# Three of four weight sums of a seven-product pair, moved from vector additions to accumulating DMA transfers

## The chip, the cores and the metric

The kernel runs on one core of a Trainium2 chip. The metric is device time in microseconds (us). A core has a matrix engine (TensorE, PE in the profile, with its weight loads shown apart as PEld), a vector engine (VectorE, DVE), a scalar engine (ScalarE, ACT), a general engine (GpSimd, POOL) and a sync engine that issues transfers (SyncE, SP). Each engine works through its own list of instructions in order; semaphores tie the lists together. Transfers are carried out by 16 DMA engines.

## The reference, cut to what matters

The program is one step of a recurrent decoder trunk with two layers over 536 token columns (16 learned tokens, 512 prompt tokens, 8 samples). Each layer has a feed-forward block, a recurrent mixer and a second feed-forward block, so there are four feed-forward blocks in all. Only they matter here:

```
def half_ffn(x, g, w_gate, w_up, w_down):
    h = rmsnorm(x, g)
    return 0.5 * ((jax.nn.silu(h @ w_gate) * (h @ w_up)) @ w_down)

x = x + half_ffn(x, norm_ffn1, ffn1_gate, ffn1_up, ffn1_down)   # D_MODEL 1024, D_FF 2816
```

All of it is 32-bit floating point.

## The kernel before, in words

The model width of 1024 is cut into 8 blocks of 128 rows, the hidden width of 2816 into 22 tiles of 128 columns. A *pair* is one such tile of the gate weights and the same tile of the up weights, 512 KB each. To keep 32-bit accuracy every operand is split into a rounded high part and the remainder (`hi` and `lo`), and a block product is three matmuls: high by high, high by low, low by high (`block_mm`, lines 330 to 337). A weight split is a cast on ScalarE (line 292) and a subtraction on VectorE that needs the cast (line 293).

Of the 22 pairs of a block the first four are *plain* (`run_plain`). The other 18 use a scheme with *seven products* in place of eight (`run_seven`, from line 471). The width is cut into two halves of 4 blocks, the tokens into two halves of 268 columns (260 in the last block), and sums and differences of halves are multiplied: sums of the activations are made once (`prepare`, tiles `sumh` and `suml`), sums of the weights for each pair. With g0, g1 the two halves of the gate tile and u0, u1 those of the up tile, the weight operands are g0 and g1 (`w`), t1 = g0 + u0, t2 = g0 + u0 + u1, s = u0 + u1, u1, and t4 = g0 + u0 + u1 + g1. A product is 12 matmuls of 128 by 128 weights and 268 columns. In order the seven products use: g0, g1, t2, t1, u0 + u1, u1, t4. They write three PSUM banks, a, b and c: the first, third, fifth and seventh product add up in a, the second stands in b, the fourth and sixth add up in c. Between them ScalarE copies an intermediate value out of a bank (`keep`, line 490), and VectorE and ScalarE finish a part of the output (lines 502, 503, 513, 516, 519). Four PSUM banks rotate.

The sums are made by `seven_item`. In the kernel before, all four are additions on VectorE into one tile `wsum` of 4 x 512 columns: `sums_a` (lines 348 and 349) makes t1 and t2, `sums_b` (lines 354 and 355) makes u0 + u1 and t4. Splits follow: `w` (1024 columns), `t` (t2 and t1, 1024 columns), `s` (u0 + u1 and t4, 1024 columns), `u` (u1, 512 columns). `it.steps` is the list of steps that the pair before calls (`nstep`), `it.late` the list of those that the pair itself calls.

The loop over pairs alternates with the down-projection: `PIECES` cuts the 22 hidden tiles into 8, 8 and 6, and behind each piece the 8 output blocks of the down-projection run over it (`run_down`). So the pairs of seven products stand in rows of 4, 8 and 6 in each of the four blocks, 72 in all.

Weights come by `load_pair` (line 300, SyncE's queue) into tiles `raw` and `rawx`, two buffers each, so that two pairs fit at a time. High and low parts go to `whi` and `wlo` or `whix` and `wlox` (`wtile`), two buffers each; a counter assigns them in turn. A tile that is asked for again waits until a buffer of its tag has been read for the last time. The order of instructions on each engine is not that of the text alone: a planner sorts what the text emits, by priority in text order and by when it takes an instruction to be ready, and then sets the semaphores.

Of the kernel before, what the change touches and what calls it, by code (L numbers as in the profile page):

```python
# [11 lines left out]
F32 = mybir.dt.float32  # L12
# [3 lines left out]
ALU = mybir.AluOpType  # L16
# [90 lines left out]
def trunk(ctx, tc, A, O):  # L107
    nc = tc.nc
    P = 128
    cnt = [0]  # L110

    def til(pool, shape, tag, dt=F32, bufs=None):
        cnt[0] += 1
        kw = {} if bufs is None else {"bufs": bufs}
        return pool.tile(shape, dt, tag=tag, name=f"{tag}_{cnt[0]}", **kw)
# [17 lines left out]
    def bank(tag="m"):  # L133
        return til(rings[tag][0], [P, 512], tag)
# [140 lines left out]
    ext = {}  # L275
    turn = {"raw": 0, "whi": 0, "wlo": 0}

    def wtile(tag):
        n = turn[tag]
        turn[tag] = n + 1  # L280
        dt = F32 if tag == "raw" else F32R
        if ext and n % 4 > 1:
            return til(ext["pool"], [P, 2, 512], f"{tag}x", dt, bufs=2)
        return til(wpool, [P, NK, P], tag, dt, bufs=2).rearrange("p (h k) m -> p h (k m)", h=2)
# [4 lines left out]
    def split_w(src):  # L289
        n = src.shape[1]  # L290
        hi, lo = wtile("whi")[:, :n], wtile("wlo")[:, :n]
        nc.scalar.copy(hi, src)
        nc.vector.tensor_sub(lo, src, hi.bitcast(F32))  # L293
        return hi, lo

    def load_pair(it, srcs, nk):
        it.raw = [wtile("raw") for _ in srcs]
        for t, src in zip(it.raw, srcs):
            dst = t.rearrange("p h (k m) -> p (h k) m", m=P)[:, :nk]
            nc.sync.dma_start(dst, src.rearrange("(k p) m -> p k m", p=P))  # L300
# [25 lines left out]
    def pair_item(wg, wu, j):  # L326
        return plain_item([w[:, 128 * j:128 * j + 128] for w in (wg, wu)], NK)


    def block_mm(o, u, nk, rh, rl, start, stop):  # L330
        hi, lo = u
        kw = {} if start else {"skip_group_check": True}
        for k in range(nk):
            nc.tensor.matmul(o, hi[:, k], rh(k), start=start and k == 0, stop=False, **kw)  # L334
            nc.tensor.matmul(o, hi[:, k], rl(k), start=False, stop=False, **kw)  # L335
            nc.tensor.matmul(o, lo[:, k], rh(k), start=False, stop=stop and k == nk - 1, **kw)  # L336
# [3 lines left out]
    def seven_item(wg, wu, j):  # L340
        it = Item()
        it.w = {}
        it.load = lambda: load_pair(it, [w[:, 128 * j:128 * j + 128] for w in (wg, wu)], NK)

        def sums_a():
            g, u = it.raw
            it.t = t = til(ext["pool"], [P, 4, 512], "wsum", bufs=1)
            nc.vector.tensor_add(t[:, 1], g[:, 0], u[:, 0])
            nc.vector.tensor_add(t[:, 0], t[:, 1], u[:, 1])

        def sums_b():
            g, u = it.raw
            t = it.t
            nc.vector.tensor_add(t[:, 2], u[:, 0], u[:, 1])
            nc.vector.tensor_add(t[:, 3], t[:, 0], g[:, 1])

        def split(name, src):
            def fn():
                it.w[name] = split_w(src())
            return fn  # L360

        it.steps = [sums_a, split("w", lambda: it.raw[0]), split("t", lambda: it.t[:, 0:2]), sums_b]
        it.late = [split("s", lambda: it.t[:, 2:4]), split("u", lambda: it.raw[1][:, 1:2])]
        return it

    def ffn(l, pre, rstd, first=None, done=None, start=None, tokens=PARTS, scaled_end=None):
# [5 lines left out]
        n = a1 - a0  # L372
        t1, t2, tl = slice(a0, a1), slice(b0, b1), slice(a0, b1)
# [6 lines left out]
        def flush():  # L380
            while pending:
                pending.pop(0)()
# [3 lines left out]
        with tc.tile_pool(name="ffn", bufs=2) as fp:  # L386
            ext["pool"] = fp

            def gtile(dt=F32):
                return til(fp, [P, 2, T], "hid", dt, bufs=9)  # L390

            def hidden(gt, ut):
                h = gtile(F32R)
                hid.append(h)

                def fn():
                    nc.vector.tensor_mul(ut[:, tl], ut[:, tl], gt[:, tl])
                    nc.scalar.copy(h[:, 0, tl], ut[:, tl])
                    nc.vector.tensor_sub(h[:, 1, tl], ut[:, tl], h[:, 0, tl].bitcast(F32))

                pending.append(fn)
# [69 lines left out]
            def run_seven(it, j, nxt):  # L471
                gt, ut = til(fp, [P, T], "gt"), til(fp, [P, T], "ut")
                bank_of = {}

                def product(b, name, i, rh, rl, first, last):
                    if first:
                        bank_of[b] = bank("d")[:, :n]
                    u = tuple(z[:, i].rearrange("p (k m) -> p k m", m=P) for z in it.w[name])
                    block_mm(bank_of[b], u, 4, rh, rl, first, last)
                    return bank_of[b]  # L480

                def half_x(h, ts):
                    return (lambda k: hh[:, 4 * h + k, ts]), (lambda k: hl[:, 4 * h + k, ts])

                def half_s(i):
                    return (lambda k: Z["h"][:, i, k]), (lambda k: Z["l"][:, i, k])

                def keep(ps):
                    s = til(fp, [P, n], "part", bufs=4)
                    nc.scalar.copy(s, ps)  # L490
                    return s

                def nstep():
                    if nxt is not None and nxt.steps:
                        nxt.steps.pop(0)()

                pa = product("a", "w", 0, *half_x(0, t1), True, True)
                s1 = keep(pa)
                it.late[0]()
                flush()  # L500
                pb = product("b", "w", 1, *half_x(1, t1), True, True)
                nc.vector.tensor_add(gt[:, t1], pb, s1)
                nc.scalar.activation(gt[:, t1], gt[:, t1], AF.Silu)
                it.late[1]()
                pa = product("a", "t", 0, *half_s(1), False, True)
                s2 = keep(pa)
                load_next()
                nstep()
                pc = product("c", "t", 1, *half_s(0), True, True)
                s3 = keep(pc)  # L510
                nstep()
                pa = product("a", "s", 0, *half_s(2), False, True)
                nc.vector.tensor_add(ut[:, t2], pa, s3)
                nstep()
                pc = product("c", "u", 0, *half_s(3), False, True)
                nc.vector.tensor_add(ut[:, t1], pc, s2)
                nstep()
                pa = product("a", "s", 1, *half_x(1, t2), False, True)
                nc.scalar.activation(gt[:, t2], pa, AF.Silu)
                hidden(gt, ut)  # L520

            def run_down(it, k0, k1, m0, parts, nxt):
                nk = k1 - k0
                flush()
                load_next()
                for i in range(2):
                    m = m0 + i
                    xv = X['x'][:, m]
                    for ts in parts:
                        sl = slice(*ts)  # L530
                        ps = bank("d")[:, :ts[1] - ts[0]]
                        block_mm(ps, it.w[i], nk, lambda k: hid[k0 + k][:, 0, sl], lambda k: hid[k0 + k][:, 1, sl],
                                 True, True)
                        nc.vector.scalar_tensor_tensor(xv[:, sl], ps, -0.5, xv[:, sl], ALU.mult, ALU.add)  # L534
                        if nxt is not None and nxt.steps:
                            nxt.steps.pop(0)()
                    if done is not None and k1 == FT:
                        late_done.append((m, parts[0]))
                        while len(late_done) > (2 if m < NK - 1 or parts[-1] != tokens[-1] else 0):
                            done(*late_done.pop(0))  # L540

            items = []
            for k0, k1 in PIECES:
                for j in range(k0, k1):
                    if j < PLAIN:
                        it = first if j == 0 and first is not None else pair_item(wg, wu, j)
# [20 lines left out]
            def load_next():  # L567
                if loads:
                    loads.pop(0).load()
# [1017 lines left out]

    xd = []
    ffn(0, "ffn1", rstd, first[0], spill(xd), loaded)
    rstd = norm_in("norm_mix", 0)  # L1590
    left.close()
    even_mixer(rstd, xd, left)
    psum(d=4, m=4)
    ffn(0, "ffn2", norm_rstd())
    xd = []
    ffn(1, "ffn1", norm_in("norm_ffn1", 1), done=spill(xd))
    rstd = norm_in("norm_mix", 1)
    left.close()
# [94 lines left out]
```

## Time and profile before

| | |
|---|---|
| median of 3 runs | 2301.66 us (2300.69 to 2308.91) |
| the profiled execution | 2313.27 us, its span 2311.5 us |
| mean granted TensorE clock | 0.991 of full speed |
| busy share of the span | TensorE 98%, weight loads 95%, VectorE 71%, ScalarE 47%, GpSimd 6% |
| mean DMA rate over the span | 99 GB/s |

The profile is of one execution. "Busy" is the time in which an engine had an instruction in work. In the list of a timeline, each instruction stands with its start, its duration, engine, line, operation and the tiles that it writes and reads (buffer numbers left out); in brackets stands how long the engine was idle before it and what ended that idle time.

### The profile page before, as it was taken

Reading aid. Unit: us, or ns where it says so; the run is one execution under the profiler, and the core shown is the slowest. Engines: PE = TensorE matmul, PEld = TensorE weight load, DVE = VectorE, ACT = ScalarE, POOL = GpSimd, SP = SyncE. Lnnn points to the kernel's source line nnn. Section 1 sums busy time; section 2 is a strip of 40 time slices with the busy share of each in tenths; the row PEclk is TensorE's granted clock in tenths of the full one; section 3 lists DMA queues with packets and bytes.
Section 4 is the critical chain, followed back from the end, with each engine's and each line's share of the span. In section 5 each row is a group of like instructions: output and inputs, shape, how many; then the busy total and the mean of one; then the engine's idle time right before and its main releaser. Section 6 shows DMA issues by size and latency. Waiting matters only on the chain.

```text
span 2311.5 us, 47443 instructions
## 1 busy us (share of the span) xinstructions
PE 2256.8 (98%) x19520; PEld 2206.5 (95%) x19520; DVE 1646.7 (71%) x2971; ACT 1082.8 (47%) x2056; POOL 143.5 (6%) x192
## 2 busy tenths in 40 slices
PE   8999999999999999999999999999999999999998
PEld 8999999998998888999999999999999889999998
DVE  7858576686666878966757885857666777948576
ACT  6525254374444456434535452525434464525355
POOL 0000000312212100000000000000021210000000
PEclk9999999999999999999999999999999999999999
DMA  6323334223222116242423332333434353333324
GB/s 171 106 78 101 92 92 132 81 64 94 79 71 72 49 49 167 74 119 75 118 74 101 92 110 74 101 92 94 128 110 128 111 160 92 92 92 101 110 85 136
DMA packets 409393, 229.23 MB, mean 99 GB/s; under 512 B 19252, under 2 KB 400501, under 8 KB 409176
## 3 DMA queue, kind: packets, MB, share of 16 engines
q1 hardware_dynamic: 408456, 224.78, 33.5%
q8 instruction: 153, 2.51, 0.5%
q10 hardware_dynamic: 720, 1.42, 0.2%
q14 instruction: 64, 0.52, 0.1%
HBM read 211.19 MB, written 14.97 MB: 98 GB/s over the span
## 4 chain that ended last, share of the span: by engine, by line
PE 86%; DVE 5%; DMA 3%; ACT 2%; issue 1%; POOL 1%; SPq 0%; ACTq 0%; POOLq 0%; DVEq 0%
PE d L334 21%; PE d L335 21%; PE d L336 21%; PE d L240 5%; PE d L242 4%; PE d L241 4%; PE w L1182 1%; PE w L1204 1%; DMA vb<-dv 1%; DVE wlo L229 1%; DMA raw<-in_even_w_out_dram 1%; PE m L155 1%; DMA sq<-dr 1%; DMA raw<-in_odd_w_out_dram 1%; PE w L1187 1%
## 5 line engine op out<-in xcount | busy, mean ns | idle before, releaser
L240 PE MATMUL d<-hh,whi 128*128 128x264 f32 (+2 forms) x1136 | 343.6, 303 | 2.0 <-DVE xT L596 1.3
L242 PE MATMUL d<-hh,wlo 128*128 128x264 f32 (+2 forms) x1136 | 326.7, 288 | 1.9 <-DVE wlo L229 1.7
L241 PE MATMUL d<-hl,whi 128*128 128x264 f32 (+2 forms) x1136 | 326.6, 288 | 0.5 <-DVE hl L1418 0.5
L334 PE MATMUL d<-hh,whi 128*128 128x268 f32 (+1 forms) x832 | 237.8, 286 | 1.8 <-ACT hh L187 1.3
L335 PE MATMUL d<-hl,whi 128*128 128x268 f32 (+1 forms) x832 | 238.1, 286 | 0.9 <-DVE hl L188 0.9
L336 PE MATMUL d<-hh,wlo 128*128 128x268 f32 (+1 forms) x832 | 237.7, 286 | 0.7 <-DVE wlo L293 0.7
L240 PEld LDWEIGHTS d<-hh,whi 128*128 128x128 f32 x1136 | 216.1, 190 | 7.5 <-issue 2.4
L242 PEld LDWEIGHTS d<-hh,wlo 128*128 128x128 f32 x1136 | 215.4, 190 | 4.6 <-DVE wlo L229 4.0
L241 PEld LDWEIGHTS d<-hl,whi 128*128 128x128 f32 x1136 | 216.3, 190 | 0.9 <-DVE hl L1418 0.7
L534 DVE SCALAR_TENSOR_TENSOR xT<-d,xT 128x272 f32<-128x272 f32 (+2 forms) x192 | 82.9, 433 | 166.7 <-PE d L336 166.6
L334 PE MATMUL d<-hid,whi 128*128 128x264 f32 (+2 forms) x704 | 201.5, 287 | 0.0
L334 PE MATMUL d<-hid,whix 128*128 128x264 f32 (+2 forms) x704 | 201.2, 286 | 0.0
L335 PE MATMUL d<-hid,whix 128*128 128x264 f32 (+2 forms) x704 | 200.8, 285 | 0.0
L335 PE MATMUL d<-hid,whi 128*128 128x264 f32 (+2 forms) x704 | 200.7, 286 | 0.0
L336 PE MATMUL d<-hid,wlox 128*128 128x264 f32 (+2 forms) x704 | 200.6, 285 | 0.0
L336 PE MATMUL d<-hid,wlo 128*128 128x264 f32 (+2 forms) x704 | 200.5, 286 | 0.0
L334 PE MATMUL d<-sumh,whix 128*128 128x268 f32 (+1 forms) x576 | 170.9, 297 | 0.0
L336 PE MATMUL d<-sumh,wlo 128*128 128x268 f32 (+1 forms) x576 | 164.7, 286 | 0.0
L335 PE MATMUL d<-suml,whix 128*128 128x268 f32 (+1 forms) x576 | 164.4, 285 | 0.0
L334 PE MATMUL d<-sumh,whi 128*128 128x268 f32 (+1 forms) x576 | 164.2, 285 | 0.0
L336 PE MATMUL d<-sumh,wlox 128*128 128x268 f32 (+1 forms) x576 | 164.0, 285 | 0.0
L335 PE MATMUL d<-suml,whi 128*128 128x268 f32 (+1 forms) x576 | 164.0, 285 | 0.0
(383 smaller groups left out, 6557.8 us busy)
## 6 DMA issues: line engine op xcount, KB each, us to landing
raw<-in_ffn_gate_dram SPq DMA_DIRECT2D x44, 512.0 KB
raw<-in_ffn_up_dram SPq DMA_DIRECT2D x44, 512.0 KB
rawx<-in_ffn_gate_dram SPq DMA_DIRECT2D x44, 512.0 KB
rawx<-in_ffn_up_dram SPq DMA_DIRECT2D x44, 512.0 KB
raw<-in_ffn_down_dram SPq DMA_DIRECT2D x32, 512.0 KB
rawx<-in_ffn_down_dram SPq DMA_DIRECT2D x32, 512.0 KB
raw<-in_even_w_in_dram SPq DMA_DIRECT2D x30, 512.0 KB
raw<-in_odd_w_in_dram SPq DMA_DIRECT2D x25, 512.0 KB
```

Source lines behind the costliest of these rows:

```text
L155: nc.tensor.matmul(ps[:, :b - a], lhsT, rhs[:, a:b], start=True, stop=True)
L229: nc.vector.tensor_sub(lo[:, ks], raw[:, ks], hi[:, ks].bitcast(F32))
L240: nc.tensor.matmul(o, hi[:, k], h, start=(k == 0), stop=False)
L241: nc.tensor.matmul(o, hi[:, k], l, start=False, stop=False)
L242: nc.tensor.matmul(o, lo[:, k], h, start=False, stop=(k == nk - 1))
L334: nc.tensor.matmul(o, hi[:, k], rh(k), start=start and k == 0, stop=False, **kw)
L335: nc.tensor.matmul(o, hi[:, k], rl(k), start=False, stop=False, **kw)
L336: nc.tensor.matmul(o, lo[:, k], rh(k), start=False, stop=stop and k == nk - 1, **kw)
L534: nc.vector.scalar_tensor_tensor(xv[:, sl], ps, -0.5, xv[:, sl], ALU.mult, ALU.add)
L1182: nc.tensor.matmul(pt[rs, 128 * i:128 * i + cs.stop], U["gm"][ks, i, rs], U["xx"][ks, i, cs], start=True, stop=True)
L1187: nc.tensor.transpose(px[:, 128 * i:128 * i + 128], U["xx"][:, i, 0:128], ident)
L1204: nc.tensor.matmul(pd[:, i], lhsT, rhs, start=True, stop=True)
```

## The change

Only the first sum, t1 = g0 + u0, stays an addition on VectorE. The other three are made by transfers from SBUF to SBUF that add to their destination, issued on GpSimd's queue (`nc.gpsimd.dma_start` with `accum_op`):

- u1 is added onto u0 within the raw up tile. The split `u` then takes the whole up tile (1024 columns): u0 + u1 and u1.
- After t1 has been split, u1 is added onto the sum tile, which then holds t2.
- After t2 has been split, g1 is added onto the same tile, which then holds t4.

The sum tile shrinks to 512 columns with the pool's two buffers. t1, t2 and t4 are split separately, 512 columns each; t1 and t2 share one pair of high and low tiles. In `run_seven` the calls move: first sum and split of t1 of the next pair stand behind the second product, the split of t4 of this pair behind the fourth, `w` of the next pair behind the sixth, t2 of the next pair behind the seventh. The products, their order and their number stay.

```diff
-        def sums_a():
-            g, u = it.raw
-            it.t = t = til(ext["pool"], [P, 4, 512], "wsum", bufs=1)
-            nc.vector.tensor_add(t[:, 1], g[:, 0], u[:, 0])
-            nc.vector.tensor_add(t[:, 0], t[:, 1], u[:, 1])
-
-        def sums_b():
-            g, u = it.raw
-            t = it.t
-            nc.vector.tensor_add(t[:, 2], u[:, 0], u[:, 1])
-            nc.vector.tensor_add(t[:, 3], t[:, 0], g[:, 1])
-
-        def split(name, src):
-            def fn():
-                it.w[name] = split_w(src())
+
+        def first_sum():
+            g, u = it.raw
+            it.t = til(ext["pool"], [P, 512], "wsum")
+            nc.vector.tensor_add(it.t, g[:, 0], u[:, 0])
+            nc.gpsimd.dma_start(u[:, 0], u[:, 1], accum_op=ALU.add)
+
+        def split(name, i):
+            def fn():
+                if i is not None:
+                    it.w[name] = split_w(it.raw[i])
+                    return
+                n = 0 if name != "t2" else 1
+                if n == 0:
+                    it.slot = wtile("whi"), wtile("wlo")
+                hi, lo = (z[:, n] for z in it.slot)
+                it.w[name] = tuple(z[:, n:n + 1] for z in it.slot)
+                nc.scalar.copy(hi, it.t)
+                nc.vector.tensor_sub(lo, it.t, hi.bitcast(F32))
+                if name != "t4":
+                    nc.gpsimd.dma_start(it.t, (it.raw[1] if name == "t1" else it.raw[0])[:, 1], accum_op=ALU.add)
             return fn
 
-        it.steps = [sums_a, split("w", lambda: it.raw[0]), split("t", lambda: it.t[:, 0:2]), sums_b]
-        it.late = [split("s", lambda: it.t[:, 2:4]), split("u", lambda: it.raw[1][:, 1:2])]
+        it.steps = [first_sum, split("t1", None), split("w", 0), split("t2", None)]
+        it.late = [split("u", 1), split("t4", None)]
         return it
...
                 nc.scalar.activation(gt[:, t1], gt[:, t1], AF.Silu)
-                it.late[1]()
-                pa = product("a", "t", 0, *half_s(1), False, True)
+                nstep()
+                nstep()
+                pa = product("a", "t2", 0, *half_s(1), False, True)
                 s2 = keep(pa)
                 load_next()
-                nstep()
-                pc = product("c", "t", 1, *half_s(0), True, True)
+                pc = product("c", "t1", 0, *half_s(0), True, True)
                 s3 = keep(pc)
-                nstep()
-                pa = product("a", "s", 0, *half_s(2), False, True)
+                it.late[1]()
+                pa = product("a", "u", 0, *half_s(2), False, True)
                 nc.vector.tensor_add(ut[:, t2], pa, s3)
                 nstep()
-                pc = product("c", "u", 0, *half_s(3), False, True)
+                pc = product("c", "u", 1, *half_s(3), False, True)
                 nc.vector.tensor_add(ut[:, t1], pc, s2)
-                nstep()
-                pa = product("a", "s", 1, *half_x(1, t2), False, True)
+                pa = product("a", "t4", 0, *half_x(1, t2), False, True)
                 nc.scalar.activation(gt[:, t2], pa, AF.Silu)
                 hidden(gt, ut)
+                nstep()
```

## Rows read from the trace of the kernel before

**Rows 1.** The page, part 1: span, and TensorE's busy time.
```profile
span 2311.5 us, 47443 instructions
...
PE 2256.8 (98%) x19520; PEld 2206.5 (95%) x19520; DVE 1646.7 (71%) x2971; ACT 1082.8 (47%) x2056; POOL 143.5 (6%) x192
```

**Rows 2.** The page, part 4: the chain that ended last, by engine.
```profile
PE 86%; DVE 5%; DMA 3%; ACT 2%; issue 1%; POOL 1%; SPq 0%; ACTq 0%; POOLq 0%; DVEq 0%
```

**Rows 3.** Busy time by windows, in a row of seven-product pairs.
```profile
core 0: us, PE busy (x) PEld busy (x) DVE busy (x) ACT busy (x) POOL busy (x), PEclk, DMA share, GB/s
...
1196.00:1238.00 42.00, 42.00 (x338) 41.71 (x337) 35.20 (x51) 24.28 (x40) 0.00 (x0) 1.00 0.33 95
```

**Rows 4.** TensorE's waits: total us, times, longest.
```profile
PE d L336 <- DVE wlo L293: 0.7, 1, 0.7
```

**Rows 5.** TensorE's timeline: start us, duration us, instruction.
```profile
1203.42 0.29 PE L334 MATMUL d<-sumh,whi 128*128 128x268 f32 x1
...
1207.77 0.28 PE L336 MATMUL d<-sumh,wlox 128*128 128x268 f32 x1
1207.91 0.39 PE L334 MATMUL d<-sumh,whix 128*128 128x268 f32 x1
1208.14 0.29 PE L335 MATMUL d<-suml,whix 128*128 128x268 f32 x1
```

**Rows 6.** ScalarE's timeline over one pair.
```profile
1202.14 0.38 ACT L490 COPY part<-d 128x268 f32<-128x268 f32 x1 [0.68 <-PE d L336]
...
1206.53 1.05 ACT L292 CAST whi<-wsum 128x1024 fp32r<-128x1024 f32 x1 [0.97 <-PE d L335]
1207.48 0.37 ACT L490 COPY part<-d 128x268 f32<-128x268 f32 x1
1209.63 1.05 ACT L292 CAST whix<-wsum 128x1024 fp32r<-128x1024 f32 x1 [1.77 <-issue]
1211.07 0.62 ACT L292 CAST whix<-raw 128x512 fp32r<-128x512 f32 x1 [0.40 <-PE d L335]
...
1212.66 0.38 ACT L490 COPY part<-d 128x268 f32<-128x268 f32 x1 [0.68 <-PE d L336]
```

**Rows 7.** Groups by line: busy us, mean ns, idle before.
```profile
L348 DVE TENSOR_TENSOR wsum<-raw,raw 128x512 f32<-128x512 f32 x36 | 24.7, 685 | 23.4 <-DMA raw<-in_ffn_up_dram 23.4
```

**Rows 8.** VectorE's timeline over one pair.
```profile
1202.57 0.68 DVE L348 TENSOR_TENSOR wsum<-raw,raw 128x512 f32<-128x512 f32 x1
1203.17 0.68 DVE L354 TENSOR_TENSOR wsum<-raw 128x512 f32<-128x512 f32 x1
...
1207.61 1.23 DVE L293 TENSOR_TENSOR wlo<-wsum,whi 128x1024 fp32r<-128x1024 f32 x1 [0.45 <-ACT whi L292]
...
1210.71 1.22 DVE L293 TENSOR_TENSOR wlox<-wsum,whix 128x1024 fp32r<-128x1024 f32 x1 [0.56 <-ACT whix L292]
1211.85 0.68 DVE L293 TENSOR_TENSOR wlox<-raw,whix 128x512 fp32r<-128x512 f32 x1
...
1213.08 0.69 DVE L348 TENSOR_TENSOR wsum<-rawx,rawx 128x512 f32<-128x512 f32 x1
```

**Rows 9.** SyncE's queue: start and duration of the issue.
```profile
1202.06 0.37 SPq L300 DMA_DIRECT2D rawx<-in_ffn_up_dram  x1
...
1212.56 0.37 SPq L300 DMA_DIRECT2D raw<-in_ffn_up_dram  x1
```

**Rows 10.** Windows of half a microsecond; the last two columns are DMA.
```profile
1202.50:1203.00 0.50, 0.50 (x6) 0.50 (x6) 0.50 (x2) 0.34 (x2) 0.00 (x0) 1.00 0.00 0
1203.00:1203.50 0.50, 0.50 (x6) 0.50 (x5) 0.50 (x2) 0.33 (x1) 0.00 (x0) 1.00 0.44 102
...
1205.50:1206.00 0.50, 0.50 (x6) 0.50 (x5) 0.50 (x1) 0.06 (x1) 0.00 (x0) 1.00 0.02 4
```

**Rows 11.** GpSimd's groups by line: busy us, mean ns, idle before.
```profile
L966 POOL TENSOR_TENSOR t<-shp,pb 128x8 f32<-128x8 f32 x14 | 11.5, 824 | 0.0
...
L1007 POOL MEMSET t<- 128x8 f32 x4 | 0.4, 104 | 31.6 <-ACT t L1002 20.0 <-ACT ws L1003 11.5
```

## The prediction

> **What bounds the kernel now.** I read the page first. TensorE is busy for 98% of the span [rows 1] and makes up 86% of the chain that ended last [rows 2]. So only work that TensorE waits for has a price. Next come the stretches of seven-product pairs, the only ones that the change touches: in 42 us of them TensorE is busy for 42.00 us at full clock, VectorE for 35.20, ScalarE for 24.28, GpSimd for nothing, and the DMA engines have a mean share of 0.33 [rows 3]. VectorE is the second most loaded engine, but a loaded engine is not a wait: in the list of what TensorE waited for, the weight splits of line 293 stand with 0.7 us once in the whole run [rows 4]. Last the pair itself. One product is 12 matmuls; the third product of a pair begins at 1203.42 and the sixth at 1207.91 [rows 5], and the whole pair repeats after 10.52 us (the copies of line 490 that take out a first product, at 1202.14 and 1212.66 [rows 6]), 1.50 us a product. I name the products P1 to P7 and count time from the start of P1, two products before 1203.42, so at 1200.42. There is one visible hole in a pair: matmuls follow each other by 0.12 to 0.13 us, but between the first and second of P6 there are 0.23 us [rows 5]. P6 adds into the PSUM bank of P4 and must wait until that bank is copied out; the copy (1207.48 [rows 6]) stood behind a 1024-column cast that began at 1206.53, just as P4 ended.
>
> **The change, part by part.**
>
> *Taken away.* Three of four additions a pair, 0.68 us each [rows 7], so 2.05 us of VectorE. Of the splits, three of 1024 columns and one of 512 become two and three: on VectorE minus 1.23 plus 2 x 0.68 us, on ScalarE minus 1.05 plus 2 x 0.62 us [rows 6, 8]. VectorE ends 1.9 us a pair lighter, ScalarE 0.2 us heavier. Neither is what TensorE waits for, so by itself this is worth nothing, with one exception: the cast that starts as P4 ends becomes 512 columns wide, 0.43 us shorter, and the copy that P6 needs comes that much earlier. That closes the 0.10 us hole: 72 x 0.10 = 7.2 us. It is nearly all that the change can gain.
>
> *Put in its place.* Three accumulating transfers of 256 KB a pair, issued on GpSimd's queue, which does nothing else there [rows 3]. The first (upper half of the up-weights onto the lower) starts with the first sum and is read only after P1 of the next pair: hidden. The other two form a chain on one tile: split t1, transfer, split t2, transfer, split t4. Let L be the time from the end of VectorE's subtraction, which frees the tile for the transfer, to the start of ScalarE's cast of the result. The trace has no accumulating transfer and none from GpSimd, so L must be bounded. A plain 512 KB load is issued at 1202.06 [rows 9]; no byte moves until 1203.0 and the engines are quiet again by 1205.5 [rows 10]: 1.0 us before the data, 2.4 us of data, 3.4 in all. Bounded below, a 256 KB transfer at that rate needs 1.0 + 1.2 = 2.2 us. But it reads two operands, 512 KB together, like the load: 3.4 us. Weight loads move data for 2 x 2.4 of each 10.5 us, and one lying wholly beside the transfer adds up to 2.4: upper bound 5.8, and I add 0.4 for a partial overlap. GpSimd's preparation lies between its smallest rows, 0.10 and 0.82 us [rows 11]; I add 0.3. So L = 4.1 us, between 2.2 and 5.8. I take a value near the 3.4 of the load because that moves the same number of read bytes.
>
> The Trainium skill speaks to this twice. "DMA: Bandwidth & Descriptors", section "Anatomy of one DMA — SWDGE (gpsimd) path", gives about 2.0 us plus the bytes at 436 GB/s for a transfer from GpSimd; for 512 KB that is 3.2 us, near the 3.4 of the load's rows, and for 256 KB an estimate of 2.6 us, by which nothing would stall (the hidden rival below). "Collectives: The Full Stack", section "The bandwidth ceiling: the fold count and why AG ≠ RS ≠ AR", says that an add inside the DMA path reads two sources and so runs at half a copy's rate; with both pages the estimate is 3.2 us, still hidden. No run so far shows an add.
>
> *Moved: the order of the splits.* Two things bind the chain. A t tile holds the split halves of t1 and t2, used in P4 and P3. It shares two buffers with the split of u, and a buffer is free when TensorE has read it: today's casts start exactly so, at 1206.53 as P4 ends and at 1209.63 as P6 ends [rows 6]. So t1 of the next pair can't be cast before the end of P4, at 6.1 us, wherever the text puts it. And the planner does not keep the text's order: the first addition of sums_b (line 354) runs right behind the first of sums_a (line 348), at 1203.17 and 1202.57 [rows 8], though products stand between the calls. It starts what is ready. The cast of t4 of this pair and the cast of t1 of the next then compete on ScalarE, which works strictly in order. t4's text stands behind t1's, but by a short planned transfer it is ready before P4 ends, so I expect it ahead of t1.
>
> That order ties the two transfers of every pair into one loop: cast t4, cast t1 of the next pair, subtract, transfer, cast t2, subtract, transfer, cast t4. Its length is 3 x 0.62 + 2 x 0.68 + about 0.1 for handovers (the subtraction at 1210.71 follows its cast by 0.03 [rows 6, 8]) + 2L = 3.3 + 2L. It fits into 10.52 us while L is at most 3.6. In the other order (t1 first) each loop holds one transfer and two products: 2 x 0.62 + 2 x 0.68 + 3.0 + 0.1 + L, which fits while L is at most 4.8. Behind a waiting cast stand, on ScalarE, the copies that free the banks for P5 and P6; so a cast that is late stalls TensorE at once, within about one product.
>
> With L = 4.1 the first loop takes 11.5 us, 1.0 more than now. The chain runs inside a row of pairs: 4, 8 and 6 pairs, so 3 + 7 + 5 = 15 repeats in each of four feed-forward blocks, 60 in all: 60 us.
>
> *Also touched.* The gate weights are held until the second transfer of the chain has landed, so their next load starts later on SP's queue. The load issued at 1202.06 is first read at 1213.08 [rows 8, 9], 11.0 us later, against 3.4 that it needs: 7 us of cover, so I cost it at nothing; without cover every microsecond of it would be paid at the first sum. The three transfers add about 3 x 2.4 us of DMA time to the 3.5 (0.33 x 10.5) that a pair uses: it still fits. The sum tile becomes two buffers of 512 columns, which only loosens waits.
>
> **The sum.** Against the profiled execution: 2313.27 us (span 2311.5, 1.8 around it) + 60 = 2373. That execution stood 11.6 us above the median of the runs, 2301.66; on the median I expect 2362.
>
> **The rivals.** *Hidden (within 0.5%).* L stays under 3.6, or the planner puts t1 first and L stays under 4.8. For it: the DMA engines idle for two thirds of the time [rows 3], and the bound of 2.2 lies well inside the budget. Against: 3.4 us, the plain load's time, nearly fills it before anything is added. Time: the hole closes, 2301.66 - 7.2 = 2294.5, or up to 2302 if it stays. Chance 0.34.
> *Faster by over 0.5%.* 11.5 us, or 0.16 us a pair, would have to come out of TensorE. The one mechanism is the hole in P6 together with the small waits at the turns from pairs to down-projections, if a lighter VectorE takes them too; the rows show 0.10 and no second hole. It decides once more than 0.16 us of a pair is found. Time about 2288. Chance 0.07.
> *The transfers collide with the loads.* An accumulating packet is served far slower than a copied one, L at the bound of 5.8: the loop is 14.9 us, 4.4 x 60 = 264, time 2565. For it: nothing measured; against: idle engines. Chance 0.07.
> *The forecast.* L between 3.7 and 5.2, a loop of 10.7 to 13.7 us. Its own range is 2315 to 2440 (+0.2 to +2.3 us a pair). Chance 0.52.
>
> **How the numbers follow.** About 0.5%, 11.5 us, is what a measurement of this kernel can tell from no change. Faster 0.07, same 0.34, slower 0.52 + 0.07 = 0.59. The time is that of the likeliest case, 2362. The range must take in the hidden case, whose low end is 2294, and reaches to 2440; below it I leave some 0.07, above it 0.11.
>
> **What would show it.** In the profile after: additions of only one kind on `wsum`, 72 of them; three accumulating transfers a pair on a GpSimd queue; on ScalarE the cast of `whi` or `whix` from `wsum` with idle time before it that ends with a DMA. If I am right, the copies of line 490's kind repeat after about 11.5 us within a row of pairs, TensorE shows a hole of about 1 us at P5, P6 or P7, and its waits name a copy on ScalarE or a split. L reads from the end of a subtraction to the next cast. If L is under 3.6 the pair stays at 10.4 us and the forecast is wrong by its largest term; if t1's cast stands ahead of t4's, the loop that I priced does not exist; if the loads land late, the first sum will wait for a DMA.

## The result, and the profile after

The changed kernel takes 2470.32 us (median of 4 runs, 2464.25 to 2472.68) beside 2303.69 us for the kernel before in the same session: a ratio of 1.0713, 95% interval 1.0696 to 1.0730. It is 167 us slower where the forecast had 60 us, and outside the range of 2294 to 2440. The line numbers of the changed kernel differ: 349 is the first sum, 350 the up transfer, 362 and 363 cast and subtraction of a split of `wsum`, 365 a transfer of the chain, 496 the copy of an intermediate value.

First the page, parts 1, 3 and 5: busy time, the queue on which GpSimd's transfers run, and one group of matmuls (busy us, mean ns, idle time before them and what ended it).

```profile
span 2470.9 us, 48139 instructions
...
PE 2305.8 (93%) x19520; PEld 2236.0 (90%) x19520; DVE 1533.1 (62%) x2827; ACT 1079.6 (44%) x2128; POOL 330.7 (13%) x408
...
q0 software_dynamic: 31104, 56.64, 13.7%
...
L334 PE MATMUL d<-sumh,whix 128*128 128x268 f32 (+1 forms) x1056 | 323.6, 306 | 105.1 <-ACT part L496 104.3
```

Against [rows 1] TensorE has the same 19520 matmuls and 49 us more busy time, but the span is 159 us longer: for the other 110 us it now waits. VectorE lost 114 us of work (the forecast's 1.9 us in 72 pairs are 137), and that bought nothing. The first matmul of a product waits for the copy of line 496. The waits say the same, and say what stands behind it (total us, times, longest):

```profile
PEld d L334 <- ACT part L496: 129.0, 108, 4.4
...
PE d L334 <- ACT part L496: 105.3, 74, 4.2
...
ACT whi L362 <- DMA wsum<-raw: 84.2, 36, 7.4
...
ACT whix L362 <- DMA wsum<-raw: 55.7, 24, 3.3
...
ACT whix L362 <- DMA wsum<-rawx: 55.2, 33, 4.8
...
ACT whi L362 <- DMA wsum<-rawx: 53.9, 26, 5.2
```

In the kernel before, the list that [rows 4] comes from has 0.7 us of waits for a subtraction of line 293 and no wait for a copy of line 490. Now ScalarE's casts wait 249 us for transfers that land in `wsum`, and the copies behind them on ScalarE hold TensorE up. One round of the loop, on ScalarE, answers to [rows 6]:

```profile
211.05 0.62 ACT L362 CAST whi<-wsum 128x512 fp32r<-128x512 f32 x1 [1.47 <-DMA wsum<-rawx]
211.57 0.38 ACT L496 COPY part<-d 128x268 f32<-128x268 f32 x1
211.84 1.05 ACT L292 CAST whi<-raw 128x1024 fp32r<-128x1024 f32 x1
212.79 0.62 ACT L362 CAST whix<-wsum 128x512 fp32r<-128x512 f32 x1
...
219.51 0.62 ACT L362 CAST whix<-wsum 128x512 fp32r<-128x512 f32 x1 [3.04 <-DMA wsum<-raw]
...
224.62 0.62 ACT L362 CAST whi<-wsum 128x512 fp32r<-128x512 f32 x1 [0.85 <-DMA wsum<-raw]
```

VectorE in the same round, which answers to [rows 8], and then GpSimd:

```profile
212.92 1.22 DVE L293 TENSOR_TENSOR wlo<-raw,whi 128x1024 fp32r<-128x1024 f32 x1 [0.53 <-ACT whi L292]
214.06 0.68 DVE L363 TENSOR_TENSOR wlox<-wsum,whix 128x512 fp32r<-128x512 f32 x1
...
220.16 0.69 DVE L363 TENSOR_TENSOR wlox<-wsum,whix 128x512 fp32r<-128x512 f32 x1 [2.44 <-ACT whix L362]
```

```profile
215.04 0.86 POOL L365 DMA_DIRECT2D wsum<-raw  x1 [7.23 <-DMA rawx<-in_ffn_up_dram]
215.99 0.86 POOL L350 DMA_DIRECT2D rawx<-rawx  x1
221.15 0.86 POOL L365 DMA_DIRECT2D wsum<-raw  x1 [4.30 <-DVE wlox L363]
```

The casts are t4 (211.05), t1 of the next pair (212.79), t2 (219.51) and t4 again (224.62): the order and the loop that the prediction named. The round takes 13.57 us where a pair took 10.52 [rows 6]. Read from the end of a subtraction to the next cast, L is 219.51 - 214.74 = 4.77 and 224.62 - 220.85 = 3.77 us. TensorE's hole at the end of this round, where P5 waits for the copy behind the cast of t4, and behind it the same place, from the last matmul of P4 to the first of P5, in the kernel before:

```profile
223.69 0.28 PE L336 MATMUL d<-sumh,wlox 128*128 128x268 f32 x1
225.57 0.39 PE L334 MATMUL d<-sumh,whix 128*128 128x268 f32 x1 [1.60 <-ACT part L496]
```

```profile
1206.28 0.29 PE L336 MATMUL d<-sumh,wlo 128*128 128x268 f32 x1
1206.41 0.29 PE L334 MATMUL d<-sumh,whix 128*128 128x268 f32 x1
```

Windows over the same round (the row of [rows 3] is its counterpart): TensorE is busy for 11.22 of 13.57 us.

```profile
211.05:224.62 13.57, 11.22 (x85) 10.55 (x84) 7.42 (x11) 5.94 (x11) 2.58 (x3) 1.00 0.61 137
```

### The profile page after: what moved, and what is told of

Its sections match the earlier page's. It is cut to its first block, busy times and chain, and to the rows that moved or that the text cites. A ratio compares the mean times of both kernels' runs of the same rounds, so it can differ in the third digit from the quotient of the medians.

```text
span 2470.9 us, 48139 instructions
## 1 busy us (share of the span) xinstructions
PE 2305.8 (93%) x19520; PEld 2236.0 (90%) x19520; DVE 1533.1 (62%) x2827; ACT 1079.6 (44%) x2128; POOL 330.7 (13%) x408
## 3 DMA queue, kind: packets, MB, share of 16 engines
q0 software_dynamic: 31104, 56.64, 13.7%
## 5 line engine op out<-in xcount | busy, mean ns | idle before, releaser
L334 PE MATMUL d<-sumh,whix 128*128 128x268 f32 (+1 forms) x1056 | 323.6, 306 | 105.1 <-ACT part L496 104.3
L334 PEld LDWEIGHTS d<-sumh,whix 128*128 128x128 f32 x1056 | 208.7, 198 | 128.1 <-ACT part L496 127.5
L335 PE MATMUL d<-suml,whix 128*128 128x268 f32 (+1 forms) x1056 | 311.8, 295 | 0.0
L336 PE MATMUL d<-sumh,wlox 128*128 128x268 f32 (+1 forms) x1056 | 311.5, 295 | 0.0
L334 PE MATMUL d<-hid,whix 128*128 128x264 f32 (+2 forms) x874 | 250.7, 287 | 6.7 <-ACT whix L292 6.7
L335 PE MATMUL d<-hid,whix 128*128 128x264 f32 (+2 forms) x874 | 249.5, 286 | 0.0
L240 PEld LDWEIGHTS d<-hh,whi 128*128 128x128 f32 x1136 | 215.7, 190 | 7.7 <-issue 2.4
L242 PEld LDWEIGHTS d<-hh,wlo 128*128 128x128 f32 x1136 | 215.2, 190 | 4.1 <-DVE wlo L229 3.4
L334 PEld LDWEIGHTS d<-hh,whi 128*128 128x128 f32 x1120 | 214.6, 192 | 4.1 <-DVE ut L519 1.8
L241 PEld LDWEIGHTS d<-hl,whi 128*128 128x128 f32 x1136 | 216.0, 190 | 0.9 <-DVE hl L1424 0.7
L335 PEld LDWEIGHTS d<-hl,whi 128*128 128x128 f32 x1120 | 214.1, 191 | 1.2 <-DVE hl L188 1.1
L336 PEld LDWEIGHTS d<-hh,wlo 128*128 128x128 f32 x1120 | 214.0, 191 | 1.0 <-DVE wlo L293 0.8
L336 PEld LDWEIGHTS d<-sumh,wlox 128*128 128x128 f32 x1056 | 209.8, 199 | 0.0
L335 PEld LDWEIGHTS d<-suml,whix 128*128 128x128 f32 x1056 | 209.6, 198 | 0.0
```

The lines of the kernel that those rows point to most:

```text
L240: nc.tensor.matmul(o, hi[:, k], h, start=(k == 0), stop=False)
L241: nc.tensor.matmul(o, hi[:, k], l, start=False, stop=False)
L242: nc.tensor.matmul(o, lo[:, k], h, start=False, stop=(k == nk - 1))
```

## The experiments

All runs, in the order in which they are told. The ratio is to the kernel before, timed beside them.

| run | what differs from the changed kernel | median us | ratio (95% interval) |
|---|---|---|---|
| e1_only_u | t2, t4 added by VectorE | 2314.4 | 1.0035 (1.0019 to 1.0051) |
| e2_no_transfer | all sums by VectorE | 2328.88 | 1.0092 (1.0070 to 1.0114) |
| e5_pin | first sum held back | 2461.23 | 1.0674 (1.0654 to 1.0694) |
| e6_no_transfer_pin | e2 and e5 | 2302.3 | 0.9991 (0.9979 to 1.0003) |
| e7_only_u_pin | e1 and e5 | 2305.24 | 0.9998 (0.9987 to 1.0009) |
| e3_t4_last | t4's cast behind t1's | 2398.9 | 1.0401 (1.0384 to 1.0419) |
| e8_t4_last_pin | e3 and e5 | 2369.75 | 1.0285 (1.0266 to 1.0304) |
| e4_w_behind | gate weights' split behind t1's | 2461.59 | 1.0669 (1.0649 to 1.0690) |
| e13_w_behind_pin | e4 and e5 | 2437.05 | 1.0569 (1.0540 to 1.0597) |
| e9_t4_last_no_u | e8, up sum by VectorE | 2333.16 | 1.0115 (1.0099 to 1.0131) |
| e14_chain_only_pin | e5, up sum by VectorE | 2446.55 | 1.0624 (1.0606 to 1.0642) |
| e15_w_behind_no_u | e13, up sum by VectorE | 2402.12 | 1.0435 (1.0389 to 1.0482) |
| e10_one_link | e5, t2 by VectorE | 2326.42 | 1.0082 (1.0056 to 1.0107) |
| e11_quarter | chain moves 128 of 512 columns | 2376.44 | 1.0301 (1.0286 to 1.0317) |
| e12_plain_copy | chain copies, doesn't add | 2399.62 | 1.0394 (1.0371 to 1.0418) |

**Which transfers cost, and what the new order costs without them.** e1 makes t2 and t4 by additions; e2 the sum of the up tile too.

```diff
-                    nc.gpsimd.dma_start(it.t, (it.raw[1] if name == "t1" else it.raw[0])[:, 1], accum_op=ALU.add)
+                    nc.vector.tensor_add(it.t, it.t, (it.raw[1] if name == "t1" else it.raw[0])[:, 1])
...
-            nc.gpsimd.dma_start(u[:, 0], u[:, 1], accum_op=ALU.add)
+            nc.vector.tensor_add(u[:, 0], u[:, 0], u[:, 1])
```

> The sums t2 and t4 are additions on VectorE again, the transfer of the up sum and the new order of the calls stay. Order theory (the loss is a loop of two transfers tied together by ScalarE's order of casts): no chain, so 2294 to 2306 us. Traffic theory (the transfers slow the loads or each other): a third of the traffic is left, about 2350. Call theory (the narrower splits and the moved calls cost by themselves): 2440 or more.

> All sums are additions on VectorE, in the new order of calls and with the narrow splits. Order theory: 2294 to 2306 us, the hole at the sixth product closed. Traffic theory: the same. Call theory: 2440 or more.

Measured: 2314.4 and 2328.88, both above the 2306 us that the order theory allowed, far below the other theories. The chain of two transfers carries nearly the whole loss; but without any transfer the new order is still slower, which was not expected. In e2, VectorE's timeline and the waits show why:

```profile
209.22 0.69 DVE L349 TENSOR_TENSOR wsum<-raw,raw 128x512 f32<-128x512 f32 x1 [0.77 <-DMA raw<-in_ffn_up_dram]
```

```profile
DVE wsum L349 <- DMA rawx<-in_ffn_up_dram: 39.6, 23, 3.7
DVE wsum L349 <- DMA raw<-in_ffn_up_dram: 37.2, 20, 3.2
...
PE d L334 <- DVE ut L519: 20.5, 26, 2.1
```

The sum tile now has two buffers, by which the planner can put the first sum of a pair early (no run took the buffer away, so that this is the reason is argued), and there it waits for the up load, 76.8 us in all where [rows 7] had 23.4. VectorE works in order, so the addition of line 519 waits behind it, and TensorE waits for that addition.

**The first sum held back.** e5, e6 and e7 order it behind the addition that follows P2; no other instruction is changed.

```diff
-                nc.vector.tensor_add(gt[:, t1], pb, s1)
+                gadd = nc.vector.tensor_add(gt[:, t1], pb, s1).ins
...
-                nstep()
+                with tc.issue_after(gadd):
+                    nstep()
```

> The changed kernel with one edit: the first sum of the next pair is pinned on VectorE behind the addition of the second product, its place in the text. Load theory (the sum tile's second buffer lets the planner put the first sum a pair earlier, where it waits for a weight load and holds up VectorE): the main part of the loss goes, about 2340 us. Loop theory (two transfers in series through ScalarE's order): that order is unchanged, so 2430 to 2470.

> No transfers, all sums on VectorE, new calls and narrow splits, first sum pinned as in the run before. Load theory: the 22 us that this order cost without the pin go, and the hole at the sixth product closes: 2296 to 2306 us. Rival (the narrow splits and moved calls themselves cost): 2320 to 2330.

> Only the up sum by a transfer, t2 and t4 on VectorE, first sum pinned. Load theory: 2296 to 2306 us. Rival (the transfer itself or its hold on the up tile costs): 2310 or more.

Measured: 2461.23, 2302.3 and 2305.24. Without transfers the pin takes away the 27 us: the order and the narrower splits cost nothing then, and e6 repeats its copies after 10.43 us. The up transfer alone is free (0.9998). With all three transfers the pin is worth only 9 us: the loop remains, as its theory said, and the theory that the late loads made the loss falls.

```profile
205.47 0.38 ACT L496 COPY part<-d 128x268 f32<-128x268 f32 x1
...
215.90 0.38 ACT L496 COPY part<-d 128x268 f32<-128x268 f32 x1
```

**Two transfers in one loop.** e3 orders t4's cast behind t1's cast and the copy of P4, so that a loop holds one transfer; e8 is e3 with the first sum held back.

```diff
-                    nc.scalar.copy(s, ps)
+                    last[0] = nc.scalar.copy(s, ps).ins
...
+                it.after["t4"] = last[0]
+                if nxt is not None and "t1" in getattr(nxt, "casts", ()):
+                    tc.add_manual_dep(last[0], nxt.casts["t1"].name, mybir.DependencyInfo(mybir.DependencyClass.NoSync, mybir.DependencyReason.DATA), reason="order")
...
-                nc.scalar.copy(hi, it.t)
+                with tc.issue_after(after) if after is not None else ExitStack():
+                    it.casts[name] = nc.scalar.copy(hi, it.t).ins
```

> All three transfers stay; only ScalarE's order is pinned: the cast of t4 stands behind the cast of t1 of the next pair and behind the copy out of the fourth product, and with it the cast of the gate weights. Order theory: one transfer a loop, 4.8 us allowed against some 4.3, so 2300 to 2330 us. Traffic theory: the traffic is as before, 2440 to 2470. Call theory: 2440 or more.

> All three transfers, t4's cast pinned behind t1's, and the first sum pinned. Loop theory with the load theory: one transfer a loop fits and no load is waited for, 2300 to 2330 us. Rival (the transfers need more than a pair allows in any order): 2370 to 2400, as without the pin.

Measured: 2398.9 and 2369.75. Both miss their theory's 2300 to 2330, e3 between its theories and e8 at the lower edge of its rival's. But from e5 to e8, where the edit touches only ScalarE's order, 91 of the 159 us between e5 and e6 are gone. What remains in e8 shows on GpSimd, SyncE and ScalarE, in this order:

```profile
212.93 0.86 POOL L351 DMA_DIRECT2D rawx<-rawx  x1 [2.14 <-DVE wsum L350]
214.39 0.86 POOL L368 DMA_DIRECT2D wsum<-rawx  x1 [0.59 <-DVE wlox L366]
```

```profile
213.43 0.37 SPq L300 DMA_DIRECT2D raw<-in_ffn_up_dram  x1
```

```profile
219.83 0.62 ACT L365 CAST whix<-wsum 128x512 fp32r<-128x512 f32 x1 [1.49 <-DMA wsum<-rawx]
```

The transfer of t1, the up transfer and the up load are issued within 1.5 us of each other, and the cast starts 5.44 us after the transfer's issue.

**The collision.** e9 is e8, e14 is e5 and e15 is e13 (below) with the up sum added by VectorE, the second edit of e2.

> As the run with t4's cast pinned last and the first sum pinned, but the up sum is an addition on VectorE again, so that only the two transfers of the chain are left. Collision theory (the up transfer is issued 1.5 us ahead of the t1 transfer and stretches it from 3.5 to 5.4 us): 2300 to 2335 us. Rival (a single transfer in the chain is too long even alone): 2355 or more.

> The changed kernel with its first sum held behind the addition of P2, and the up sum added on VectorE instead of by a transfer; the two transfers of the chain and the planner's order on ScalarE stay. Collision theory: the up transfer and the loads behind it lengthen the landings of the chain here as they did with t4 last (37 us there), so 2410 to 2435. Rival: in this order the up transfer runs beside no transfer of the chain, and the time stays at 2450 to 2465.

Measured: 2333.16 and 2446.55. With t4 last the up transfer costs 37 us, in the planner's own order 15, which lies between e14's two theories and nearer to the rival. The landings go with that: in e8, 100 of the 144 transfers of the chain have an up transfer in flight at some time between their issue and their landing, and land after 4.44 us on the mean, the other 44 after 3.83; in e5 71 have one, and they land after 3.71 us like the rest. The 31 us between e9 and e6 are what the two transfers cost in the better order without it.

**The fixed part of the loop.** e4 orders the split of the next gate weights behind t1's cast; e13 does that with the first sum held back.

```diff
-                    it.w[name] = split_w(it.raw[i])
+                    with tc.issue_after(it.casts["t1"]) if name == "w" and "t1" in it.casts else ExitStack():
+                        it.w[name] = split_w(it.raw[i])
```

> All three transfers stay, t4 stays ahead of t1, but the gate weights' cast is pinned behind the cast of t1. Order theory: the loop loses that cast (0.95 us) and the subtraction that held t1's (some 0.6), so 1.5 us less in each of 60 repeats, 2470 - 90 = 2380 us (2350 to 2400). Traffic theory: 2460 to 2475. Call theory: 2440 or more.

> The changed kernel with its first sum held behind the addition of P2 on VectorE, and the split of the next block's gate weights held behind the cast of t1 on ScalarE (t4 is still cast first). Loop theory: the split of the gate weights stands inside the loop of the two transfers (its cast on ScalarE about 0.95 us, its subtraction on VectorE ahead of t1's), so moving it out takes about 0.95 to 1.5 us from each of some 60 rounds: 57 to 90 us below the 2461 of the pinned planner's order, 2370 to 2405. Rival: the split only filled time in which t1 waited for something else (VectorE or the copy of P4), and the time stays at 2445 to 2465.

> The run with the gate weights' split held behind t1's cast and the first sum held behind P2, and now also the up sum added on VectorE instead of by a transfer. There the loop's fixed part had fallen from 5.05 to 3.5 us, and the mean stretch from a subtraction's end to the next cast had risen from 4.15 to 4.64 us, the long stretches being those of the transfers issued 3.4 us or less after an up transfer and 2.5 us after an up load. Collision theory: with the up transfer gone the stretch falls back to about 4.1 us, the loop to 3.5 + 8.2 = 11.7 us, and the time to 2375 to 2400. Rival: the load alone lengthens the stretch as much, and the time stays at 2415 to 2437.

Measured: 2461.59, 2437.05 and 2402.12. e4 missed the order theory and lies in the range of the two others; it moved the wait: its first sum waits 115.7 us for the up loads (65.9 and 49.8), that of the changed kernel 65.5 (33.2 and 32.3). In e13 ScalarE's order is as wanted, and the time falls by only 24 us, between the two theories:

```profile
207.04 0.62 ACT L366 CAST whi<-wsum 128x512 fp32r<-128x512 f32 x1 [1.32 <-DMA wsum<-rawx]
207.57 0.38 ACT L500 COPY part<-d 128x268 f32<-128x268 f32 x1
207.84 0.62 ACT L366 CAST whix<-wsum 128x512 fp32r<-128x512 f32 x1
...
214.40 0.62 ACT L366 CAST whix<-wsum 128x512 fp32r<-128x512 f32 x1 [2.20 <-DMA wsum<-raw]
```

The casts of all 60 repeats show where the time goes. A round runs from one cast of t4 to the next; L is taken from the end of each subtraction of t1 and t2 to the next cast of the chain; the rest of the round is its fixed part. Means over the 60 rounds of each kernel, from the timelines of ScalarE and VectorE; which sum a cast belongs to is read from the tile that it writes and, for t1 and t2, from the transfer that is issued behind its subtraction:

| run | round us | fixed part (median) | L | 60 x (round - 10.42) | span less e6's 2299.7 |
|---|---|---|---|---|---|
| changed kernel | 13.34 | 4.80 (5.05) | 4.27 | 175 | 171 |
| e5_pin | 13.16 | 4.89 (5.05) | 4.14 | 164 | 161 |
| e13_w_behind_pin | 12.73 | 3.99 (3.87) | 4.37 | 139 | 135 |
| e15_w_behind_no_u | 12.25 | 3.80 (3.49) | 4.22 | 110 | 102 |
| e6_no_transfer_pin | 10.42 | | | 0 | 0 |

The fixed part fell by 0.90 us when the split moved (e5 to e13), and the two transfers, each 0.23 us longer, took 0.46 of it back. Part of that is the up transfer: without it (e13 to e15) a round is 0.48 us shorter, 2 x 0.15 in L and 0.19 in the fixed part, and the time 35 us. Without it on both sides, the move of the split takes 44 us (e14 to e15). Both theories for e13 had one number each for a sum of two that pull against each other; for e15 the collision theory was 2 us off its upper end, and the 4.64 us that it names for e13's stretch are 4.37 over all 60 rounds. The last two columns agree within 8 us, so the rounds are where the loss is.

In the changed kernel the cast of t1 stands ahead of the cast of t4 in 11 of the 60 rounds, each the first of a row of pairs. One such place on ScalarE, and the transfer that GpSimd issues between the two casts:

```profile
168.07 0.62 ACT L362 CAST whix<-wsum 128x512 fp32r<-128x512 f32 x1 [4.92 <-PE d L335]
...
170.98 0.62 ACT L362 CAST whi<-wsum 128x512 fp32r<-128x512 f32 x1 [0.97 <-PE d L335]
```

```profile
169.71 0.86 POOL L365 DMA_DIRECT2D wsum<-rawx  x1 [10.73 <-DVE wlox L363]
```

The transfer marks the cast at 168.07 as t1's of the next pair; that of t4 follows. Over the 12 rows the first rounds take 9.23 us and the second ones 17.55 on the mean, against 12.37 and 13.86 in e5, whose t4 is ahead in all 60. From the third round on the two kernels are nearly equal: 13.31 and 13.19 us, the fixed part 5.04 and 5.02. So e5's pin shortens the rounds by 0.18 x 60 = 11 us, and the time by 9.

**The transfer's own length.** e10 has one transfer in the chain: t2 by VectorE, t4 by transfer. e11 moves only the first 128 of 512 columns in the chain, so the rest of t2 and t4 lacks its addend. e12 copies in the chain in place of adding, so t2 is u1 and t4 is g1.

```diff
+                    if name == "t1":
+                        nc.vector.tensor_add(it.t, it.t, it.raw[1][:, 1])
+                    else:
+                        nc.gpsimd.dma_start(it.t, it.raw[0][:, 1], accum_op=ALU.add)
...
+                    nc.gpsimd.dma_start(it.t[:, 0:128], (it.raw[1] if name == "t1" else it.raw[0])[:, 1, 0:128], accum_op=ALU.add)
...
+                    nc.gpsimd.dma_start(it.t, (it.raw[1] if name == "t1" else it.raw[0])[:, 1])
```

> Changed kernel with the first sum pinned; t2 is an addition on VectorE, t4 and the up sum are transfers. ScalarE's order is left to the planner. Loop theory: one transfer a turn, some 9.7 us, under 10.5: 2300 to 2325 us. Rival (each transfer that a cast waits for costs its share): half of the loss, 2380.

> Changed kernel, but the two transfers of the chain add only the first 128 of 512 columns; three quarters of t2 and t4 are left out. Loop theory: whatever a transfer gets shorter counts twice a turn; if data make up 1.2 us of it, 0.9 us less each, 1.8 x 60 = 108, so 2360 us (2330 to 2400). Rival (a transfer's time is fixed cost): 2450 to 2470.

> Changed kernel, but the two transfers of the chain copy instead of add, so t2 and t4 hold the wrong values. ScalarE's and VectorE's orders are the same. If the second operand that an add reads costs 0.6 us of data time: 1.2 x 60 = 72 us less, 2400 us (2380 to 2420). If an add costs no more than a copy: 2455 to 2475.

Measured: 2326.42, just above what was expected, and 2376.44 and 2399.62, as expected. With one link the loop nearly fits; and a shorter landing takes time off round by round: L is 3.48 in e11 and 3.73 in e12 in place of 4.27, over 120 links 95 and 65 us, and the times fell by 94 and 71. A quarter of the bytes doesn't bring a quarter of the landing: the median falls from 3.6 to 2.8 us. From issue to landing, in the tile's view of the changed kernel, of e11 and of e12:

```profile
DMA to landing us min/median/max: 3.2/3.6/6.5
```

```profile
DMA to landing us min/median/max: 2.3/2.8/5.0
```

```profile
DMA to landing us min/median/max: 2.2/3.3/5.6
```

The Trainium skill's "Collectives: The Full Stack", section "The bandwidth ceiling: the fold count and why AG ≠ RS ≠ AR", says of the reduce step of a ring collective that its add reads two sources and so runs at half the rate of the copying step. The shortest landings here, 3.2 us for an add against 2.2 for a copy, go the same way; the medians, 3.6 and 3.3, are nearer to each other.

## Why the prediction was right and wrong

*Right: the order and the loop.* The planner did put t4's cast ahead of t1's of the next pair in 49 of the 60 rounds, and there the two transfers of a pair did close into one loop; in 11 first rounds of a row t1's stood ahead. The copies behind the late casts stall TensorE at once. From e5 to e8 ScalarE's order alone moves 91 us.

*Right: L.* The estimate was 4.1 us; the mean over 120 links is 4.27, in e5 4.14. The parts fit too: in e5 0.32 us from the subtraction to the issue, 3.76 from issue to landing and 0.05 to the cast, where the sum had 0.3 for GpSimd and 3.4 + 0.4 for the transfer.

*Wrong, and the failed step: the loop's fixed part.* The prediction summed 3 x 0.62 + 2 x 0.68 + 0.1 = 3.3 us. It let the cast of t1 follow the cast of t4, and each subtraction its cast. In the round shown, t1's cast starts 1.74 us after t4's, in place of 0.62: between them stand the copy (0.27 until the next starts) and the cast of the next gate weights (0.95). And t1's subtraction ends 1.95 us after its cast began, in place of 1.3, since the gate weights' subtraction of 1.22 us is ahead of it. Together 1.12 + 0.65 = 1.77 us, which makes 5.07; the median is 5.05. The 1.75 us that the median is longer than the forecast are 105 us in 60 rounds, beside the 107 by which the time was under-forecast. The prediction did see the copies behind a late cast, as what stalls TensorE, but not as a part of the loop. e13 shows the term: with the split out of the way the fixed part is 3.99, median 3.87. It also shows that the term's price is not its length: in the 36 rounds from the third on, the fixed part falls from 5.02 (e5) to 3.61 us, but each L grows from 4.09 to 4.45, so that 0.67 us a round and 24 us in all are gained. Why L grows is not settled; in e13 the 91 transfers of the chain that meet an up transfer land after 3.88 us on the mean, the other 53 after 3.84.

*Wrong: "two buffers, which only loosens waits", and loads at nothing.* The first sum, which can now run early, waits 65.5 us for the up loads in the changed kernel where it waited 23.4 before [rows 7], and at the heads of rows it lets t1's cast pass t4's. The rounds are 0.18 us longer on the mean than with the sum held back (e5), 11 us by these numbers, 9 measured: small here, but 27 us in e2, where nothing else is wrong.

*Wrong: a sum of the range.* The forecast's own case was a loop of 10.7 to 13.7 us. By its own rule that is up to 13.7 - 10.5 = 3.2 us a pair, 192 us in 60 repeats and a time of 2494; the text has 2.3 us and 2440. The measured round of 13.34 us lies inside that case, the time outside the range that was given for it.

*Wrong: the up transfer as hidden.* It is free alone (e7), and costs 15 to 37 us beside the chain. The prediction had weighed weight loads against the chain, not the third transfer of the same pair.

*The 7 us of the hole.* The rounds of e6 are 10.42 us in place of 10.52, which over 72 pairs is 7 us; the whole kernel came out 2 us faster, an interval that includes no change. In the changed kernel the loop is longer than TensorE's work, so the hole was never the limit.

So 60 us had been forecast as 60 x (11.5 - 10.5). The rounds of the changed kernel are 13.34, 1.8 us longer than 11.5: 1.5 in the mean of the fixed part and 0.3 in the two L. The rule that an L under 3.6 would hide the chain falls with it: with 5.05 in place of 3.3 the bound is (10.5 - 5.05) / 2 = 2.7 us, and no landing of a 256 KB add was under 3.2.

What stays open, beside the growth of L in e13: why e3 and e8 missed their 2300, and why e9 stays 31 us above e6. In e9, TensorE waits 17.4 us for copies, and the landings of its chain still reach 6.1 us; the parts of the 31 us were not taken apart.

## What to carry to other kernels

When a wait becomes a loop, list every instruction that stands between its members on each in-order engine, from the planned order and not from the source: here a split that belongs to another operand made the loop 1.8 us longer, and moving it out gave back only 24 to 44 us, as the transfers then took longer. An addition of 0.68 us on an engine that nobody waits for is a bad trade for a transfer of 3.2 to 6.5 us inside a chain; the one transfer with a whole pair of slack cost nothing. An instruction that a planner can put early may cost time: it then runs into a wait, in front of others that were ready.

## What the runs showed of the hardware that was not expected

*An add cost its issuer more.* A transfer of the chain occupies GpSimd for 0.86 us when it adds (median 862 and 859 ns) and 0.54 to 0.55 us when it copies (e12). On the queue, the same 56.64 MB take 13.7% of 16 engines' span in the changed kernel, and 9.3% in e12, whose chain copies. They go in 31104 packets against 21888: 144 for an add of 256 KB, 80 for a copy.

*Landings were longer beside other traffic on the DMA engines, even beside one packet of instructions.* Two transfers of e15 with the same neighbours, in the DMA view of the 8 us from 203 and of the 6 us from 216 (queue: packets, MB, share; then median us to landing):

```profile
q1 hardware_dynamic: 1040, 0.52, 22.7%
q0 software_dynamic: 144, 0.26, 19.3%
q8 instruction: 1, 0.02, 0.7%
...
wsum<-raw POOLq DMA_DIRECT2D x1, 256.0 KB, 5.1
```

```profile
q1 hardware_dynamic: 1040, 0.52, 29.6%
q0 software_dynamic: 144, 0.26, 25.1%
...
wsum<-rawx POOLq DMA_DIRECT2D x1, 256.0 KB, 3.3
```

The first has a packet of the instruction queue in it and lands 1.8 us later. Over the 144 transfers of e15's chain, taken one by one from issue to landing: 38 with fewer than 300 load packets and no packet of queue q8, mean 3.33 us; 40 with 700 or more load packets and none of q8, 4.11; 8 with 700 or more and one of q8, 5.41. A long landing has more time to meet packets; counted over the first 3.2 us of each alone, the three groups are 51, 41 and 7 transfers, with means of 3.44, 4.15 and 5.36. In the changed kernel the 108 without a packet of q8 have a mean of 3.65 and the 36 with one 4.37. This is an association; no run took the instruction packets away. The Trainium skill's "DMA: Bandwidth & Descriptors", section "Queues, rings and completion order", says that a DMA engine serves its queues in turn, a packet at a time, and that a transfer's signal lands only after every earlier write of that engine; the counts go the way that this would take them.

*The clock fell behind a long hole.* Windows of 4 us of the changed kernel (the last three numbers are granted clock, DMA share, GB/s):

```profile
196.00:200.00 4.00, 1.07 (x7) 1.07 (x8) 0.83 (x2) 2.02 (x4) 0.00 (x0) 0.97 0.17 46
200.00:204.00 4.00, 4.00 (x22) 4.00 (x22) 2.95 (x5) 1.04 (x3) 1.72 (x2) 0.61 0.46 119
204.00:208.00 4.00, 4.00 (x35) 4.00 (x34) 2.70 (x5) 2.57 (x5) 0.86 (x1) 1.00 0.77 149
```

After a window with 1.07 us of matmuls the granted clock is 0.61, mostly the lower of its two levels, and TensorE does 22 matmuls where it does 35 at full clock. Over the run the clock is 0.979 against 0.991 before. No run isolates what this cost; the members of the loop run on ScalarE, VectorE and the DMA engines, not on TensorE.
